# A four-mixer block on one core: bias rows spread by four transfers, memory tokens prepared in pieces, earlier splits of the last weights, another closing chain

## The chip, the cores and the metric

The kernel runs on one core of one Trainium2 chip. The metric is device microseconds (us) of one execution. The engines are named as in the profile: PE (matrix products), PEld (its weight loads), DVE (vector), ACT (scalar), POOL (GpSimd) and SP, whose queue (SPq) issues the transfers (DMA).

## The reference, cut to what matters

All inputs are fp32, one sequence of 512 tokens, model width 1024, 256 memory tokens.

```
h = _rmsnorm(x, norm_g[l])
p_fox, p_ssm, p_nsa, p_mem = _split(h @ w_in[l], [FOX_COLS, SSM_COLS, NSA_COLS, MEM_COLS])
mem_kv = _rmsnorm(mem, mem_norm_g[l]) @ w_mem_kv[l]
o = concatenate([_fox_mixer(p_fox, ..), _ssd_mixer(p_ssm, ..), _nsa_mixer(p_nsa, .., rel_bias_table), _mem_mixer(p_mem, mem_kv)])
x = x + o @ w_out[l]
return _rmsnorm(x, final_norm_g)
```

fox is causal attention with a decay, ssd a scan over state in four chunks of 128 tokens, nsa attention over compressed, selected and windowed keys with a bias taken from a table by distance, mem attention to the memory tokens. Inside ssd the lines that the change touches are

```
y = _ssd_chunked(xs * dt, dt * a, bh, ch)
y = y + xs * d_skip
yg = y * silu(z)
return _rmsnorm(yg by groups of 256, norm_g)
```

where a chunk's result is `cb @ x`, inside the chunk, plus `C @ prev * exp(acs)`, with `prev` the state that the chunks before left.

## The kernel before, in words

**Precision.** Every large product is made of three: each operand is split into a high part, rounded to a shorter format, and the low rest. A tile of weights (`raw`, 128x1024, 512 KB) arrives by a transfer on SP, ACT copies it into `wh` and POOL subtracts to get `wl` (`split`). `three` then issues `wh*hh`, `wh*hl` and `wl*hh`. Rings of three hold `raw`, `wh` and `wl`. The last output weights (`wo1`, eight halves) are split into `lh` and `ll`, which lie in the general store.

**Order.** `ORDER` lists 74 weight tiles. Tiles are taken in that order. While the Python code is run to emit instructions, a planner (`Clock`) keeps an estimated time for every engine, `Sched` and `Pipe` pick the next step by it: weight tiles are filled in where the pipeline steps of the mixers (fox, cmp, mem, pre, ssm, nsa, each a `Pipe` of stages) would wait. So the order of instructions on every engine is fixed when the program is built, and each engine takes its own list in order. `tt` puts an elementwise product on DVE or on POOL by the planner's estimate. `Store` counts the tiles that are free: 51 of 128x512 (`gs`) and 12 of 128x1024 (`bs`). A pipeline keeps some in reserve (RF, RM, RN, RS) and holds at most so many steps open (DF, DM, DN, DS).

**Start.** `proj_b("bv")` makes fox's values from the unscaled, unnormalised tokens `uh`/`ul` (ACT, DVE), tile by tile as `xt` arrives: per tile two row blocks k of 128, four token tiles each.

**Bias of nsa.** `rel_bias` makes eight rows `rv`, writes them to DRAM, and eight transfers DRAM to DRAM copy each row 128 times (`rows`, 328 KB each). Much later `bias_tile` reads the copies with a step that is one element shorter, so that each partition has a shifted row.

**Memory tokens.** `mem_r` and `prep_mem` normalise: `prm` on PE spreads a factor, DVE makes `mt`, ACT `mh`, POOL `ml`. `mem_v` multiplies them with the `mv` weights into `pmv`. In the list of things to do, the preparation is an entry (`memx`) right ahead of the first `mv`.

**The scan.** For each chunk stage s1 makes `pR`, `pG`, `pX` (and `pB`) on PE, two masks `m` from `pR` on DVE, `ce` and eight exponentials on ACT, `m*pG` on DVE, and `xdt`, `xde`. Then `pst` and `prev` (the state), `pY` on PE (32 products from the second chunk on), `yc` on DVE (four from `pY`, four times z), its squares `sq` on ACT, sums by `pn` on PE, and after `rsr`/`prs` the scaled `of`, split to `oh`/`ol`. `po` are the output products. `wo1` needs the scan's `oh`/`ol`.

**Close.** `out_last` adds the last `po` to `acc` by pieces, and `finish` squares on ACT with a running sum, adds it up through `fv` and `fw` (DVE), takes the power (`fr`, POOL), multiplies by the gain `fgn`, scales half on DVE and half on ACT, and two transfers write 128 tokens.

Every instruction is recorded at the line of one helper (L229 before, L231 after), so rows are told apart by tile names.

## Time and profile before

| | us |
|---|---|
| median of 3 runs | 564.74 (563.86 to 565.84) |
| the profiled execution | 564.22 |
| its span in the profile | 562.4 |
| PE busy in it | 545.1 (97%) |
| DVE, ACT, POOL busy | 335.2, 316.0, 228.0 |

The span is divided between times at which the engines work and short stretches at which PE does nothing. Times in the rows below count from the span's start. A timeline row has the start, the duration, the engine, the operation with what it writes and reads, how many such follow one another, and in brackets the idle time just ahead of it and what ended that.

### The profile page before, as it was taken

Reading aid. Unit: us, or ns where it says so; the run is one execution under the profiler, and the core shown is the slowest. Engines: PE = TensorE matmul, PEld = TensorE weight load, DVE = VectorE, ACT = ScalarE, POOL = GpSimd, SP = SyncE. Lnnn points to the kernel's source line nnn. Section 1 sums busy time; section 2 is a strip of 40 time slices with the busy share of each in tenths; the row PEclk is TensorE's granted clock in tenths of the full one; section 3 lists DMA queues with packets and bytes.
Section 4 is the critical chain, followed back from the end, with each engine's and each line's share of the span. In section 5 each row is a group of like instructions: output and inputs, shape, how many; then the busy total and the mean of one; then the engine's idle time right before and its main releaser. Section 6 shows DMA issues by size and latency. Waiting matters only on the chain.

```text
span 562.4 us, 8836 instructions
## 1 busy us (share of the span) xinstructions
PE 545.1 (97%) x3237; PEld 450.5 (80%) x3237; DVE 335.2 (60%) x891; ACT 316.0 (56%) x709; POOL 228.0 (41%) x145
## 2 busy tenths in 40 slices
PE   8999979999989999999999999999999999999993
PEld 4897858887867888888888888888888888888683
DVE  3566555665565354555646656777666556778654
ACT  5656534876456554556655657556656563527323
POOL 3495342332658334333131423333133313739433
PEclk9999979999989999999999999999999999999997
DMA  8772462212614232513221222442212211223012
GB/s 289 305 260 89 177 197 99 76 26 70 226 38 143 89 106 76 175 53 109 80 76 38 75 76 76 139 163 76 75 38 76 75 60 54 76 75 114 1 38 112
DMA packets 18919, 59.01 MB, mean 105 GB/s; under 512 B 2315, under 2 KB 2587, under 8 KB 18876
## 3 DMA queue, kind: packets, MB, share of 16 engines
...
q8 instruction: 25, 0.41, 0.3%
q14 instruction: 18, 0.15, 0.1%
...
## 4 chain that ended last, share of the span: by engine, by line
PE 84%; DVE 4%; DMA 3%; issue 3%; POOL 2%; ACT 2%; SPq 1%; POOLq 0%; ACTq 0%; DVEq 0%
PE pj L229 41%; PE po L229 12%; PE pO L229 7%; PE pT L229 6%; PE pb L229 6%; PE pS L229 5%; DMA raw<-in_wst 3%; PE pmv L229 2%; PE pW L229 1%; PE pY L229 1%; SPq L229 1%; DVE acc L229 1%; ACT sq L229 1%; POOL ll L229 1%; POOL fr L229 0%
## 5 line engine op out<-in xcount | busy, mean ns | idle before, releaser
L229 POOL TENSOR_TENSOR wl<-raw,wh 128x1024 fp32r<-128x1024 f32 (+1 forms) x72 | 172.2, 2396 | 283.4 <-ACT wh L229 262.6
L229 PE MATMUL pj<-hh,wh 128*128 128x512 f32 x352 | 144.4, 410 | 2.2 <-ACT wh L229 2.2
L229 PE MATMUL pj<-hh,wl 128*128 128x512 f32 x352 | 138.9, 395 | 1.2 <-POOL wl L229 1.2
L229 PE MATMUL pj<-hl,wh 128*128 128x512 f32 x352 | 138.7, 394 | 0.0
L229 ACT ACTIVATE wh<-raw 128x1024 fp32r<-128x1024 f32 (+1 forms) x72 | 74.9, 1042 | 21.5 <-DMA raw<-in_wst 14.4
L229 PEld LDWEIGHTS pj<-hh,wl 128*128 128x128 f32 x352 | 66.6, 189 | 16.7 <-POOL wl L229 1.9
L229 PEld LDWEIGHTS pj<-hh,wh 128*128 128x128 f32 x352 | 66.9, 190 | 15.9 <-ACT wh L229 2.6
L229 PEld LDWEIGHTS pj<-hl,wh 128*128 128x128 f32 x352 | 67.0, 190 | 10.7
L229 ACT ACTIVATE pN<-pN,nm 128x128 f32<-128x128 f32 (+7 forms) x96 | 45.3, 473 | 30.6 <-DVE nm L229 29.7
L229 PE MATMUL po<-wh,oh 128*128 128x512 f32 x96 | 39.4, 410 | 0.0
L229 PE MATMUL po<-wh,ol 128*128 128x512 f32 x96 | 37.6, 391 | 0.0
L229 PE MATMUL po<-wl,oh 128*128 128x512 f32 x96 | 37.5, 391 | 0.0
L229 ACT ACTIVATE pN<-pN,rs 128x128 f32<-128x128 f32 (+3 forms) x32 | 18.1, 564 | 29.0 <-DVE rs L229 29.0
L229 DVE TENSOR_SCALAR rs<-sm 128x3 f32<-128x3 f32 x32 | 11.9, 371 | 28.1 <-ACT pN L229 28.1
L229 DVE CUSTOM_DVE_ANT_0 pN<-pS,bt 128x128 f32<-128x128 f32 (+4 forms) x72 | 21.0, 329 | 12.1 <-PE pS L229 10.3
L229 ACT ACTIVATE pF<-pF,nm 128x128 f32<-128x128 f32 (+3 forms) x32 | 17.7, 554 | 14.6 <-DVE nm L229 14.6
L229 DVE SCALAR_TENSOR_TENSOR xs<-cb,cwh,xs 128x512 f32<-128x512 f32 x24 | 18.0, 752 | 11.5 <-ACT xs L229 10.9
L229 DVE TENSOR_TENSOR acc<-acc,po 128x512 f32<-128x512 f32 (+1 forms) x33 | 21.2, 665 | 5.4 <-PE po L229 5.4
L229 DVE COPY pt<-pT 128x512 f32<-128x512 f32 (+1 forms) x37 | 21.8, 599 | 3.1 <-PE pT L229 2.9
L229 PE MATMUL pT<-cst,pN 128*128 128x128 f32 x160 | 23.0, 275 | 0.0
L229 PE MATMUL pb<-wh,ul 128*128 128x512 f32 (+1 forms) x64 | 21.4, 347 | 0.8 <-DVE ul L229 0.8
L229 PEld LDWEIGHTS pT<-cst,pN 128*128 128x128 f32 x160 | 18.7, 140 | 4.3 <-issue 1.2
...
## 6 DMA issues: line engine op xcount, KB each, us to landing
...
```

The lines of the kernel that those rows point to most:

```text
L229: return f(*a, **k)
```

## The change

- `proj_b("bv")`: per tile the order of products is now hh, ul for the first row block, hh for the second, `wl` for the first, ul and `wl` for the second. Before, hh and ul alternated for both row blocks, then `wl`.
- Bias rows: four transfers of 656 KB (256 rows), two when `rv` is written, the others at nsa's steps 0 and 1. `bias_tile` is one transfer in place of two. `rel` follows `kc`, which is nine places later in `ORDER`.
- Memory tokens: a generator in `side`, stepped once each time an `mv` or `mk` tile is among the next three things to do. `mem_v` and `mk` run what is left of it.
- `wo1` weights may be split four tiles ahead (others two, as before).
- The scan: the factor 0.5 is moved into two small vectors, so that `yc` times z is a plain product which `tt` can place on POOL.
- Close: sums of pieces in one tile `fs`, one reduction, POOL multiplies the first half by the gain, one DVE instruction applies factor and gain to the second half, ACT scales the first. The end of a token tile is emitted behind the next tile's first addition. The last transfer is issued by ACT.
- Numbers: `ORDER`, depths, reserves and the biases of `tt` are others (two of ORDER's lines are shown), and the planner counts 2.0 us more for a PE step ahead of which PE stood for over 1.7 us.

```diff
-DF, DM, DN, DS = 4, 6, 3, 4
+DF, DM, DN, DS = 5, 3, 5, 3
...
-RF, RM, RN, RS = 3, 2, 2, 4
-
-SOON, LATER, WIDE = 0, 2500, 8000
+RF, RM, RN, RS = 4, 3, 2, 7
+
...
-    ("kc", 0), ("fq", 1), ("fg", 0), ("fk", 0), ("fk", 1), ("fq", 2), ("fg", 1), ("fk", 2),
...
+    ("fk", 0), ("fk", 2), ("vc", 0), ("fq", 3), ("fg", 0), ("fk", 1), ("fq", 1), ("fq", 2),
...
     def can_split():
         i = state["split"]
-        if i >= min(state["next"] + 2, len(ORDER)):
+        if i >= len(ORDER) or i >= state["next"] + (4 if ORDER[i][0] == f"wo{LAST}" else 2):
...
             ks_ = range(i * per, min((i + 1) * per, KT))
-            for x, w_ in (("h", h_), ("l", l_)):
-                for k in ks_:
-                    if name == "bv" and (i, x) in (((0, "h"), (0, "l"))[1:] + ((1, "h"),)):
-                        stat_x(k)
-                    ahead()
-                    if name == "bc" or i > 1:
-                        pump()
-                    cs = slice((k - i * per) * width, (k - i * per + 1) * width)
-                    for t in range(4):
-                        tk = slice(t * 128, (t + 1) * 128)
-                        if x == "h":
-                            T.matmul(pb[t][:, :width], uh[k][:, tk], w_[:, cs], start=k == 0, stop=False)
-                            T.matmul(pb[t][:, :width], ul[k][:, tk], w_[:, cs], start=False, stop=False)
-                        else:
-                            T.matmul(pb[t][:, :width], uh[k][:, tk], w_[:, cs], start=False, stop=k == KT - 1)
+            if name == "bv":
+                order = [(0, 0), (0, 1), (1, 0), (0, 2), (1, 1), (1, 2)]
+            else:
+                order = [(j, x) for j in range(len(ks_)) for x in (0, 1)] + [(j, 2) for j in range(len(ks_))]
+            for n_, (j, x) in enumerate(order):
+                k = ks_[j]
+                if name == "bv" and (i, n_) in ((0, 3), (0, 5), (1, 1), (1, 3)):
+                    stat_x(2 * i + n_ // (5 - 2 * i))
+                ahead()
+                if name == "bc" or i > 1:
+                    pump()
+                cs = slice(j * width, (j + 1) * width)
+                u, w_ = (ul if x == 1 else uh)[k], l_ if x == 2 else h_
+                for t in range(4):
+                    T.matmul(pb[t][:, :width], u[:, t * 128:(t + 1) * 128], w_[:, cs],
+                             start=k == 0 and x == 0, stop=k == KT - 1 and x == 2)
             done((h_, l_))
...
+    side = []
+
+    def memory(whole=False):
+
+        while side and side[0]:
+            if next(side[0], 1):
+                side[0] = None
+            if not whole:
+                break
+
     def soon(key):
+        if key[0] in ("mv", "mk") and (len(mh) or bg.room(4 + bg.kept(), 2)):
+            memory()
...
     def tile_a(key, sink, h=None, width=512):
         h_, l_ = get(key)
-        yield max(clock.ready([h_, l_]), clock.free_banks(1))
+        if h:
+            memory(True)
+        hi, lo = h if h else (hh, hl)
+        yield max(clock.ready([h_, l_, *hi, *lo]), clock.free_banks(1))
         p = PS("pj")
-        hi, lo = h if h else (hh, hl)
...
         cs = slice(c0, c0 + w)
-        sq, fs = G("sq", FT, w), SM("fs", 1)
-        A.activation(sq, a[:, cs], AF.Square, accum_out=fs)
+        if i == 0:
+            fin["s"] = SM("fs", 4)
+            V.memset(fin["s"], EPS)
+        fs = fin["s"]
+        sq = G("sq", FT, w)
+        A.activation(sq, a[:, cs], AF.Square, scale=D ** -0.5, accum_out=fs[:, i:i + 1])
         gs.drop()
-        if not last:
-            tt(LATER, out=a[:, cs], in0=a[:, cs], in1=g[:, cs], op=OP.mult)
-            if i == 0:
-                fin["v"] = SM("fv", 1)
-                V.tensor_scalar(out=fin["v"], in0=fs, scalar1=1.0 / D, scalar2=EPS, op0=OP.mult, op1=OP.add)
-            else:
-                V.scalar_tensor_tensor(out=fin["v"], in0=fs, scalar=1.0 / D, in1=fin["v"], op0=OP.mult, op1=OP.add)
+        if i == 0:
+            P.tensor_tensor(out=a[:, cs], in0=a[:, cs], in1=g[:, cs], op=OP.mult)
+        if last:
+            fin["end"] = t, i, fs
+
+    def end():
+        if "end" not in fin:
             return
+        t, i, fs = fin.pop("end")
+        a, g = acc[t], fin["g"]
         v, r = SM("fw", 1), SM("fr", 1)
-        V.scalar_tensor_tensor(out=v, in0=fs, scalar=1.0 / D, in1=fin["v"], op0=OP.mult, op1=OP.add)
+        V.tensor_reduce(out=v, in_=fs[:, 0:i + 2], axis=mybir.AxisListType.X, op=OP.add)
         P.tensor_tensor(out=r, in0=v, in1=nhalf[:, :1], op=OP.pow)
-        V.tensor_tensor(out=a[:, cs], in0=a[:, cs], in1=g[:, cs], op=OP.mult)
-        V.tensor_scalar(out=a[:, 0:512], in0=a[:, 0:512], scalar1=r, scalar2=None, op0=OP.mult)
-        Q.dma_start(out=out[t][:, 0:512], in_=a[:, 0:512])
-        A.activation(a[:, 512:1024], a[:, 512:1024], AF.Copy, scale=r)
+        V.scalar_tensor_tensor(out=a[:, 512:1024], in0=a[:, 512:1024], scalar=r, in1=g[:, 512:1024],
+                               op0=OP.mult, op1=OP.mult)
         Q.dma_start(out=out[t][:, 512:1024], in_=a[:, 512:1024])
+        A.activation(a[:, 0:512], a[:, 0:512], AF.Copy, scale=r)
+        (Q if t < 3 else nc.scalar).dma_start(out=out[t][:, 0:512], in_=a[:, 0:512])
...
             V.tensor_tensor(out=a, in0=a, in1=p[:, :w], op=OP.add)
+            end()
             finish(t, i, c0, w, i == len(pieces) - 1)
...
-    rows = [[dr.tile([128, RVW], FT, name=f"rows{j}_{a}") for a in range(2)] for j in range(4)]
+    rows = [dr.tile([2, 128, RVW], FT, name=f"rows{j}") for j in range(4)]
...
-        for j in range(4):
-            for a in range(2):
-                src = rv[4 * a + j:4 * a + j + 1, :]
-                Q.dma_start(out=rows[j][a], in_=bass.AP(tensor=src.tensor, offset=src.offset,
-                                                              ap=[[0, 128], [1, RVW]]))
-            yield 0
+        yield 0
         gs.drop(2)
         bs.drop()
+        spread(0)
+        spread(1)
+
+    def spread(j):
+        src = rv[j:j + 1, :]
+        Q.dma_start(out=rows[j], in_=bass.AP(tensor=src.tensor, offset=src.offset, ap=[[4 * RVW, 2], [0, 128], [1, RVW]]))
 
     def bias_tile(j):
         t = B4("bt", [128, 2, BTW])
-        for a in range(2):
-            src = rows[j][a]
-            Q.dma_start(out=t[:, a, :], in_=bass.AP(tensor=src.tensor, offset=src.offset + 127,
-                                                          ap=[[RVW - 1, 128], [1, BTW]]))
+        src = rows[j]
+        Q.dma_start(out=t, in_=bass.AP(tensor=src.tensor, offset=src.offset + 127,
+                                       ap=[[RVW - 1, 128], [128 * RVW, 2], [1, BTW]]))
         return t
...
                     bts[j + 1] = bias_tile(j + 1)
+                if j < 2:
+                    spread(j + 2)
...
-                V.scalar_tensor_tensor(out=yc[:, jc], in0=xs[j][:, ck], scalar=v_d[:, j:j + 1], in1=po[:, jc],
+                V.scalar_tensor_tensor(out=yc[:, jc], in0=xs[j][:, ck], scalar=hd[:, j:j + 1], in1=po[:, jc],
                                        op0=OP.mult, op1=OP.add)
             for j in range(4):
                 jc = slice(j * 128, (j + 1) * 128)
-                V.scalar_tensor_tensor(out=yc[:, jc], in0=yc[:, jc], scalar=0.5, in1=R["z", j][:, ck],
-                                       op0=OP.mult, op1=OP.mult)
+                tt(0, out=yc[:, jc], in0=yc[:, jc], in1=R["z", j][:, ck], op=OP.mult)
...
     def mem_v():
+        memory(True)
         for i in range(4):
             h_, l_ = get(("mv", i))
-            yield max(clock.ready([h_, l_]), clock.free_banks(2) if i == 0 else 0.0)
+            yield max(clock.ready([h_, l_, *mh, *ml]), clock.free_banks(2) if i == 0 else 0.0)
...
-    rm = mem_r()
+    side.append(prep_mem(mem_r()))
...
-        if key[0] in ("mv", "mk") and not seen_x:
-            bg.add(("memx", 0), prep_mem(rm))
-            seen_x = True
```

SP's queue where the bias rows are copied. First before: `rv` are the eight rows, `rows` the copies, `raw` weight tiles.

```order
L229 DMA raw<-in_wst 128x1024
L229 DMA rv<-rvs 8x328
L229 DMA rv<-rvt 8x328
L229 DMA rows_0_487<-rv 128x656
L229 DMA rows_1_488<-rv 128x656
L229 DMA rows_0_489<-rv 128x656
L229 DMA rows_1_490<-rv 128x656
L229 DMA rows_0_491<-rv 128x656
L229 DMA rows_1_492<-rv 128x656
L229 DMA rows_0_493<-rv 128x656
L229 DMA rows_1_494<-rv 128x656
```

The same place after; `xst` are small transfers of compressed keys.

```order
L231 DMA raw<-in_wst 128x1024 x4
L231 DMA xst<-kv 64x511
L231 DMA xst<-kv 64x512
L231 DMA raw<-in_wst 128x1024 x6
L231 DMA rv<-rvs 8x328
L231 DMA rv<-rvt 8x328
L231 DMA rows_487<-rv 256x1x656
L231 DMA rows_488<-rv 256x1x656
L231 DMA raw<-in_wst 128x1024
L231 DMA xst<-kv 64x511
```

The copies stand behind nine more weight tiles, and two transfers are left here.

PE's queue at the memory tokens, before. `pcm` are products of the compression, `prm` and `pmv` as above.

```order
L229 MATMUL pcm_1573<-w1_1511,xp_1519 64x128
L229 MATMUL pcm_1573<-w1_1515,xp_1525 64x128
L229 MATMUL prm_1609<-cst_98,rmr_546 128x128 x2
L229 MATMUL pmv_1640<-wh_1437,mh_1613 128x512
L229 MATMUL pmv_1640<-wl_1438,mh_1613 128x512
L229 MATMUL pmv_1640<-wh_1437,ml_1612 128x512
```

After, at `prm` (`pj` are products of ordinary weight tiles):

```order
L231 MATMUL pj_1429<-hl_435,wh_1206 128x512
L231 MATMUL pj_1429<-hh_413,wl_1207 128x512
L231 MATMUL prm_1523<-cst_98,rmr_542 128x128 x2
L231 MATMUL pj_1543<-hh_276,wh_1292 128x512
L231 MATMUL pj_1543<-hl_298,wh_1292 128x512
```

and at `pmv`:

```order
L231 MATMUL pj_1632<-hh_413,wh_1425 128x512
L231 MATMUL pj_1632<-hl_435,wh_1425 128x512
L231 MATMUL pj_1632<-hh_413,wl_1426 128x512
L231 MATMUL pmv_1673<-wh_1534,mh_1527 128x512
L231 MATMUL pmv_1673<-wl_1535,mh_1527 128x512
L231 MATMUL pmv_1673<-wh_1534,ml_1526 128x512
```

Between `prm` and `pmv` there now stand 48 products `pj` (two weight tiles) and 32 of `pcm`.

PE's queue at the last chunk of the scan, before, from the `pst` ahead of that chunk's `pR` to the first `pY` of the third chunk:

```order
L229 MATMUL pst<-xde,bt 128x256 x2
L229 MATMUL pR<-bd,cgs 128x512 x2
L229 MATMUL pG<-xs 128x128 x2
L229 MATMUL pX<-cst,xs 128x128 x4
L229 MATMUL po<-wh,oh 128x512
L229 MATMUL po<-wl,oh 128x512
L229 MATMUL po<-wh,ol 128x512
L229 MATMUL po<-wh,oh 128x512
L229 MATMUL po<-wl,oh 128x512
L229 MATMUL po<-wh,ol 128x512
L229 MATMUL prs<-cst,rsr 128x128 x2
L229 MATMUL pY<-m,xdt 64x128 x2
```

This `pY` is followed by 12 `po`, the last chunk's `pY`, 15 `po`, and then `pn`. After, from the last `po` ahead of the last chunk's `pR`:

```order
L231 MATMUL po<-wh,ol 128x512
L231 MATMUL pR<-bd,cgs 128x512 x2
L231 MATMUL pG<-xs 128x128 x2
L231 MATMUL pX<-cst,xs 128x128 x4
L231 MATMUL pst<-xde,bt 128x256 x2
L231 MATMUL pY<-m,xdt 64x128 x2
L231 MATMUL pY<-ce,prev 64x128 x2
```

The pair of `pY` rows stands eight times, four for the third chunk and four for the last, and behind them:

```order
L231 MATMUL pY<-m,xdt 64x128 x2
L231 MATMUL pY<-ce,prev 64x128 x2
L231 MATMUL pn<-ones,sq 128x1 x2
L231 MATMUL po<-lh,oh 128x512
L231 MATMUL po<-ll,oh 128x512
L231 MATMUL po<-lh,ol 128x512
```

The `po` with `lh` are the first of `wo1`. Ahead of the first row of after stand the third chunk's `pR`, `pG`, `pX`, `pB` and eight more `po`; between the two chunks' `pR` there were 30 `po` before and are nine now, and no product of another kind stands between the last `pR` and `wo1`.

DVE's queue there, before, from the last chunk's masks on:

```order
L229 TENSOR_TENSOR m<-pR,umask 128x512 x2
L229 TENSOR_TENSOR xdt<-pX,dtv 128x512
L229 TENSOR_TENSOR m<-m,pG 128x512 x2
L229 SCALAR_TENSOR_TENSOR of<-yc,vec,prs 128x128 x4
L229 TENSOR_TENSOR ol<-of,oh 128x512
L229 SCALAR_TENSOR_TENSOR yc<-xs,vec,pY 128x128 x4
L229 SCALAR_TENSOR_TENSOR yc<-yc,sg 128x128 x4
L229 TENSOR_TENSOR sq<-sq 128x128
L229 SCALAR_TENSOR_TENSOR yc<-xs,vec,pY 128x128 x4
L229 SCALAR_TENSOR_TENSOR yc<-yc,sg 128x128 x4
```

After, from the third chunk's `xdt` on:

```order
L231 TENSOR_TENSOR xdt<-pX,dtv 128x512
L231 TENSOR_TENSOR xde<-xdt,dte 128x512
L231 TENSOR_TENSOR m<-m,pG 128x512 x2
L231 TENSOR_TENSOR acc<-acc,po 128x512 x2
L231 TENSOR_TENSOR m<-pR,umask 128x512 x2
L231 TENSOR_TENSOR xdt<-pX,dtv 128x512
L231 TENSOR_TENSOR m<-m,pG 128x512 x2
L231 TENSOR_TENSOR prev<-prev,decR 128x512
L231 TENSOR_TENSOR prev<-prev,pst 128x512
L231 SCALAR_TENSOR_TENSOR yc<-xs,hd,pY 128x128 x4
L231 TENSOR_TENSOR yc<-yc,sg 128x128
```

The last chunk's masks stand behind the third chunk's `m*pG`, and the third chunk's `yc` behind the last chunk's `m*pG` and `prev`.

## Rows read from the trace of the kernel before

**Rows 1.** The chain of work that ended last, from the page: shares of the span by engine.

```profile
PE 84%; DVE 4%; DMA 3%; issue 3%; POOL 2%; ACT 2%; SPq 1%; POOLq 0%; ACTq 0%; DVEq 0%
```

**Rows 2.** Busy time of the engines by stretch: start and end, length, then for PE, PEld, DVE, ACT, POOL the busy us and in brackets the instructions; then PE's granted clock as a share of full speed, the share of the DMA engines, and GB/s.

```profile
75.00:77.50 2.50, 0.68 (x4) 0.22 (x2) 0.00 (x0) 0.74 (x1) 0.00 (x0) 1.00 0.52 199
77.50:85.00 7.50, 5.92 (x14) 4.25 (x15) 4.00 (x5) 3.50 (x5) 7.02 (x3) 0.54 0.44 143
...
159.00:163.00 4.00, 1.70 (x9) 1.06 (x8) 3.97 (x10) 2.13 (x4) 1.57 (x2) 1.00 0.00 0
163.00:166.50 3.50, 3.50 (x12) 2.95 (x12) 1.65 (x7) 2.75 (x7) 3.50 (x4) 0.51 0.00 0
166.50:529.00 362.50, 362.50 (x2240) 304.44 (x2240) 220.76 (x639) 206.37 (x496) 139.03 (x83) 1.00 0.25 85
529.00:531.70 2.70, 2.14 (x10) 1.32 (x9) 2.15 (x5) 2.56 (x6) 2.32 (x3) 1.00 0.00 0
531.70:535.20 3.50, 3.45 (x9) 1.73 (x7) 0.82 (x3) 0.54 (x2) 3.50 (x3) 0.51 0.00 0
```

**Rows 3.** Timeline of PE and of DVE in the first tile of `bv`.

```profile
8.09 0.40 PE L229 MATMUL pb<-wh,ul 128*128 128x512 f32 x1
8.32 0.43 PE L229 MATMUL pb<-wh,uh 128*128 128x512 f32 x1
9.55 0.50 PE L229 MATMUL pb<-wh,ul 128*128 128x512 f32 x1 [0.80 <-DVE ul L229]
...
8.23 1.92 DVE L229 SCALAR_TENSOR_TENSOR ul<-xt,vec,uh 128x512 fp32r<-128x512 f32 x2 [1.70 <-ACT uh L229]
```

**Rows 4.** Timeline of SP's queue where the bias rows are copied.

```profile
58.76 5.75 SPq L229 DMA_DIRECT2D rows<-rv  x8
64.61 1.29 SPq L229 DMA_DIRECT2D raw<-in_wst  x1
```

**Rows 5.** Timeline where the weights behind them land.

```profile
76.76 1.06 ACT L229 ACTIVATE wh<-raw 128x1024 fp32r<-128x1024 f32 x1 [5.88 <-DMA raw<-in_wst]
...
77.87 0.80 PE L229 MATMUL pj<-hh,wh 128*128 128x512 f32 x1 [2.18 <-ACT wh L229]
```

**Rows 6.** Timeline of PE, DVE and POOL at the memory tokens.

```profile
161.35 0.50 PE L229 MATMUL pmv<-wh,mh 128*128 128x512 f32 x1 [1.63 <-ACT mh L229]
...
162.76 0.56 PE L229 MATMUL pmv<-wh,ml 128*128 128x512 f32 x1 [0.68 <-POOL ml L229]
...
159.78 3.21 DVE L229 SCALAR_TENSOR_TENSOR mt<-mt,vec,prm 128x256 f32<-128x256 f32 x8
...
161.43 4.99 POOL L229 TENSOR_TENSOR ml<-mt,mh 128x512 fp32r<-128x512 f32 x4 [6.59 <-issue]
```

**Rows 7.** Timeline of PE and POOL at the last weight tile of `wo1`.

```profile
531.23 0.50 PE L229 MATMUL po<-ll,oh 128*128 128x512 f32 x1 [0.52 <-POOL ll L229]
...
529.90 5.44 POOL L229 TENSOR_TENSOR ll<-raw,lh 128x512 fp32r<-128x512 f32 x4
```

**Rows 8.** Timeline of the scan's last chunk: PE's block `pR` to `pX` (the next `po` ends it), the state `prev`, the masks and the last `m*pG`; PE's `pY` of that length, from its first row to the next `po`; `yc`, its squares, and their sums.

```profile
514.58 0.81 PE L229 MATMUL pR<-bd,cgs 128*128 128x512 f32 x2
514.71 0.97 DVE L229 TENSOR_TENSOR prev<-prev,decR 128x512 f32<-128x512 f32 x1
...
515.78 0.69 DVE L229 TENSOR_TENSOR prev<-prev,pst 128x512 f32<-128x512 f32 x1
...
516.03 0.48 PE L229 MATMUL po<-wh,oh 128*128 128x512 f32 x1
...
516.39 1.28 DVE L229 TENSOR_TENSOR m<-pR,umask 128x512 f32<-128x512 f32 x2
...
520.73 0.69 DVE L229 TENSOR_TENSOR m<-m,pG 128x512 f32<-128x512 f32 x1 [0.49 <-ACT m L229]
...
522.89 0.44 PE L229 MATMUL pY<-m,xdt 128*64 128x128 f32 x4
...
524.78 0.50 PE L229 MATMUL po<-wh,oh 128*128 128x512 f32 x1
...
526.71 1.12 DVE L229 SCALAR_TENSOR_TENSOR yc<-xs,vec,pY 128x128 f32<-128x128 f32 x4
...
528.67 0.63 ACT L229 ACTIVATE sq<-yc 128x512 f32<-128x512 f32 x1 [2.20 <-DVE yc L229]
...
529.38 0.56 POOL L229 TENSOR_TENSOR sq<-sq 128x128 f32<-128x128 f32 x1 [2.27 <-ACT sq L229]
```

**Rows 9.** The tile `xde`: one DVE operation with two inputs, three times; ns shortest, median and longest.

```profile
L229 DVE TENSOR_TENSOR xde<-xdt,dte x3: 693/1298/1811, 470.8 to 508.4; 128x512 f32<-128x512 f32 x3
```

**Rows 10.** Timeline of the close, from PE's last product.

```profile
553.28 0.28 PE L229 MATMUL po<-lh,ol 128*128 128x256 f32 x1
...
555.06 0.15 DVE L229 TENSOR_SCALAR fv<-fs 128x1 f32<-128x1 f32 x1 [0.85 <-ACT sq L229]
...
556.31 0.41 DVE L229 TENSOR_TENSOR acc<-acc,po 128x256 f32<-128x256 f32 x1
...
557.60 0.59 POOL L229 TENSOR_TENSOR fr<-fw,nhalf 128x1 f32<-128x1 f32 x1 [0.55 <-DVE fw L229]
...
558.23 0.49 DVE L229 TENSOR_SCALAR acc<-acc,fr 128x512 f32<-128x512 f32 x1 [0.43 <-POOL fr L229]
558.74 0.81 SPq L229 DMA_DIRECT2D out<-acc  x2
```

More of the change, by code (lines that the diff above doesn't have):

```diff
@@ L144, in note @@
                 self.tiled = tiled
+            if start > self.t[eng] + 1700:
+                took += 2000
         elif eng == "SP":
-            took = 430
+            took = 720 if self.box(out) == (0, 1, 0, 1) else 430
         elif eng == "ACT":
@@ L169, in note @@
             nbytes = 4 * self.size(out) * out.ap[0][1]
-            self.dma = max(self.dma, done) + nbytes / 340
+            self.dma = max(self.dma, done) + nbytes / (170 if took > 430 else 340)
             done = self.dma + 2100
@@ L263, in step @@
         item = self.todo[0]
-        if item[2] is None:
-            for key, *_ in self.todo[:2]:
-                self.soon(key)
+        for key, *_ in self.todo[:3]:
+            self.soon(key)
         try:
@@ L618, in block_kernel @@
     gs.drop(16)
+    mh, ml = [], []
     o_f, o_hl, last = {}, {}, [0]
@@ L623, in ready @@
         g, b = TAKES[key[0]]
+        if key[0] in ("mv", "mk") and not mh:
+            g, b = g + 4, b + 2
         if key[0] in ("ks", "kw") and kx or key[0][:2] == "wo" and acc:
@@ L1372, in s1 @@
                 xde = G("xde")
-                V.tensor_tensor(out=xde.rearrange("p (h d) -> p h d", h=8),
-                                in0=xdt.rearrange("p (h d) -> p h d", h=8), in1=hb(dte, c), op=OP.mult)
+                tt(SOON, out=xde.rearrange("p (h d) -> p h d", h=8),
+                   in0=xdt.rearrange("p (h d) -> p h d", h=8), in1=hb(dte, c), op=OP.mult)
             for g in range(2):
@@ L1604, in block_kernel @@
     adders.update(extra)
-    seen_mv = seen_x = False
+    seen_mv = False
     for key in ORDER[7:]:
-        if key[0] in ("mv", "mk") and not seen_x:
-            bg.add(("memx", 0), prep_mem(rm))
-            seen_x = True
         if key == ("kc", 0):
@@ L1629, in block_kernel @@
         bg.fill()
+    end()
 def _bucket(dist):
```

12 lines of the change are left out of this document (7 added, 5 removed), and 12 rows, old and new, of the table ORDER.

## The prediction

> **What bounds the kernel now.** I read the chain of waits first. PE has 84% of it, no other engine more than 4% [rows 1]: the time is PE's work plus the places where PE stands or runs slowly. So I looked for these places in the busy times by stretch. In the long middle PE is busy for all of 362.5 us at full clock [rows 2]; the loss lies in a few short stretches and at the two ends. In a stretch I count as lost PE's idle time, and of its busy time the share that the granted clock lacks. Three stretches come out:
>
> - 75.0 to 85.0: idle 1.82 + 1.58, and 5.92 busy at 0.54 loses 2.7, sum 6.1 us. PE waits for `wh`, ACT had waited 5.88 us for a weight tile [rows 5]. That tile was issued at 64.61, behind eight copies of bias rows which took SP 5.75 us [rows 4].
> - 159.0 to 166.5: idle 2.30, and 3.50 at 0.51 loses 1.7, sum 4.0. PE waits 1.63 for `mh` and 0.68 for `ml`: DVE, ACT and POOL prepare memory tokens that PE wants at once [rows 6].
> - 529.0 to 535.2: idle 0.61, and 3.45 at 0.51 loses 1.7, sum 2.3. `ll` of the last tile is made while PE is there [rows 7]; modelled ends of products hide a little, I take 2.5.
>
> A clock near 0.5 of 2.4 GHz is the lower level, 1.2; each time it follows an idle gap of PE in the same stretch or the one before. At the start one wait for `ul` moves a product from 0.23 to 1.23 us behind the last [rows 3]. At the end 9.1 us pass from PE's last product at 553.28 to the span's end, 562.4.
>
> **The change part by part.** *Start.* The product at 8.32 is the ninth, the one at 9.55 the tenth and the first to read `ul` of the second block, which DVE has ready just ahead of it (the first of the two from 8.23) [rows 3]. In the new order that `ul` is first read by the seventeenth product, at 8.32 + 8 × 0.23 = 10.2, so the wait of 1.0 goes. The weight tiles that follow then have 1.0 less room, so between 0 and 1.0 is gained; I take 1.0, since nothing is added to ACT or POOL there.
>
> *Bias rows.* Two transfers of 656 KB at this place carry half the bytes, so SP and the queue behind them should be done in about half of the time that the eight took: the weight tile that landed 12.1 us after its issue (64.61 to 76.76 less a little) would take some 6. By the order, with 0.23 a product, its split is due about 17 us after the place of the copies and its use about 33. That covers it twice. The other two transfers stand at nsa's steps 0 and 1, alone. Gain 6.1; with the cover gone, up to 6.1 comes back. `bias_tile` in one transfer saves SP an issue; SP bounds nothing there.
>
> *Memory tokens.* Between `prm` and the first `pmv` PE has 48 products `pj`, 48 × 0.23 = 11.0 us, and 32 `pcm`. The preparation took from 159.78 (DVE) to 166.4 (end of POOL's four `ml`), 6.6 us, and POOL's weight splits for two tiles can be put between. It is hidden with over 4 us to spare: gain 4.0. If POOL were late after all, that comes back.
>
> *Last weights.* Made up to four tiles ahead, `ll` is ready well before PE is there: gain 2.5.
>
> *The price: the last chunks.* `wo1` held early takes 16 tiles of the general store, and with the larger reserve of the scan (RS 7) the last two chunks start late. The order shows what that does: behind the third chunk's `pR` stand nine `po`, the last chunk's `pR`, both `pY`, `pn`, then `wo1`. PE has nothing else to run while two chunks go one behind the other through DVE and ACT, where before 12 and 15 `po` stood in between. Durations of [rows 8], with zero at the third chunk's `pR`:
>
> 1. PE: `pR` to `pX` 1.45 twice, `pB` 0.15, nine `po` 2.05, `pst` 0.7 (about three products): 5.8. Two `pY` of 1.9 and `pn` would end at 9.75 if nothing had to be waited for.
> 2. DVE: the third chunk's masks start at about 1.0 (behind `of` and `ol` in its order). From masks to the end of the last `m*pG` it is 516.39 to 521.42, 5.03. ACT also copies `bt`, some 0.2 more: end 6.2. Two additions `acc` of 0.65 follow: 7.5.
> 3. Then the last chunk's masks: 7.5 + 5.03 = 12.5. `prev` 514.71 to 516.47, 1.76: 14.3. The last `pY` reads it and runs from 14.3 to 16.2, or to 18.1 at half clock.
> 4. Only then, in DVE's order, the third chunk's `yc`: 14.3 + 1.1. Of its products by z three go to POOL, 0.56 each like the sums of squares there, from 14.65 to 16.35. Squares on ACT 0.7: 17.05. Sum on POOL 0.56: 17.6. `pn`, and `wo1` can start at 17.8 to 18.3.
>
> That is 8.0 to 8.5 behind 9.75; I take 8.2. PE stands about 6 us in one piece in it, so a stretch at half clock follows; the three of before lasted 3.5 to 7.5 us and lost 1.7 to 2.7 each [rows 2]. Part of it lies under `pY`, which is waited out anyway. I add 1.5, from 0 to 3.5. Sum 9.7, between 8 and 12; more, by 1 to 1.5, if DVE comes to the third chunk's masks late because four `acc` stand ahead.
>
> Eleven of sixteen products by z are on POOL. The one row that bears on the two engines together is `xde`, two inputs from SBUF, the same shape three times: 693, 1298 and 1811 ns [rows 9]; something holds it up by as much as 1.1. I count no such hold-up in the steps above. The Trainium skill (SBUF — State Buffer, section "SBUF: two separate sides") says that DVE and POOL share one pair of ports, that a DVE operation with two inputs from SBUF or a POOL operation takes it for its whole length, and that the other is blocked entirely. The spread of `xde` agrees. By that rule two of the three products on POOL could each cost DVE 0.56 more, and the forecast would be 1.1 later.
>
> *Close.* Before, the last addition on DVE stood behind `fv`, which waited for ACT, and started at 556.31, 3.0 after PE's last product [rows 10]. Now no such wait is ahead of it: it can start 0.5 after (product 0.28, and a little). From addition to the second half's scaling it was 556.31 to 558.23, 1.9, the same steps now (squares, a sum, power); the scaling is one operation with gain, about 0.2 longer. The transfer issue 0.4 later is saved, since ACT issues the other. So 2.5 − 0.2 + 0.4 less a little for the power on POOL, which also holds a product by the gain: 2.4, between 1.8 and 2.7.
>
> *Sum.* Gains 1.0 + 6.1 + 4.0 + 2.5 + 2.4 = 16.0, price 9.7. The profiled execution is 564.22 (span 562.4, 1.8 around it), so 557.9. The median is 0.52 above it: **558.4**.
>
> **The rivals.**
>
> *A, the forecast:* 555 to 561.5.
>
> *B, the last chunks cost less* (3 to 7): the 5.03 from masks to the last `m*pG` holds waits, since other work of that time stood between (`ce` on ACT among it). If a chunk takes 3.5 with nothing beside it, twice 1.5 is saved, and with a shorter gap the half clock: 558.4 − 3.0 − 1.5 = 553.9, so 551 to 555.5. Against it: `ce` is made in every chunk, and `prev` stood ahead of the masks in the row, so the 5.03 holds none of it.
>
> *C, a smaller stall elsewhere*, where preparation in pieces makes `wl` late (POOL has 5.0 of `ml` beside 2 × 2.4 of `wl` in 11 us), or the shorter start leaves a `bv` tile late. It gives back 3 to 6: 561.5 to 564.5. Against it: POOL was idle for 14.5 us at a time in the profile.
>
> *D, the copies still block a weight tile:* the bytes are the same in all, and a transfer of 656 KB may hold the queues as long as two of 328. One such stall as before gives back 6.1: 564.5, no change. That is also the case in which the change doesn't do what it says.
>
> *E, slower:* the same mechanism at three places, the pair and the two single transfers in nsa's steps, each ahead of a weight tile. At 6.1 a place it is 558.4 + 18.3 = 576.7; it decides from the second place on, with 570.6 for two. For it: 5.88 us of waiting were seen behind eight copies. Against it: each single transfer is a quarter of that, and three weight tiles are kept in the ring.
>
> **How the numbers follow.** A 0.60, B 0.11, C 0.12, D 0.09, E 0.08. A measurement of this kernel can tell about 0.3%, 1.7 us, from no change. Faster by more than that is below 563.05: A, B and most of C, 0.80. Within it: D and the rest of C, 0.12. Slower: E, 0.08. The range leaves out E, part of D and the lower half of B: 552 to 564.
>
> **What would show it.** Right: in the changed profile the first `bv` tile without the gap of 1.23; ACT without a wait of several us for a weight tile behind `rows`; `pmv` without waits; no wait of `po` for `ll`; the span's end 6.5 to 7 us after PE's last product. And one stretch near the end, just ahead of the first `po` with `lh`, in which PE idles for 8 us between `pY` and `pn` with DVE on `m*pG` and `prev`, followed by a granted clock near 0.5. Wrong: `pY` of the last chunk released at once (B), PE idle behind `rows` (D, E), or `wl` late beside `ml` (C).

## The result, and the profile after

| | before | changed |
|---|---|---|
| median, us | 564.46 (563.86 to 565.84, 4 runs) | 571.83 (570.55 to 574.34, 4 runs) |
| ratio, 95% interval | | 1.0132 (1.0091 to 1.0174) |
| profiled execution (span) | 564.22 (562.4) | 571.07 (568.9) |

The change made the kernel 1.3% slower; 558.4 was forecast, and 552 to 564 as the range. The chain that ended last, from the page of the changed kernel, answers to [rows 1]:

```profile
PE 79%; DVE 7%; ACT 6%; DMA 6%; issue 1%; POOL 0%; SPq 0%; POOLq 0%; DVEq 0%; ACTq 0%
```

DMA has doubled, ACT tripled, and PE lost 5 points. The stretches of the changed kernel, columns as in [rows 2]:

```profile
143.00:146.00 3.00, 0.80 (x7) 0.41 (x6) 0.00 (x0) 0.00 (x0) 0.00 (x0) 0.95 0.82 233
146.00:160.00 14.00, 4.22 (x27) 3.66 (x28) 0.00 (x0) 1.80 (x3) 4.46 (x6) 0.52 0.67 240
160.00:521.80 361.80, 361.80 (x2235) 304.12 (x2234) 217.92 (x620) 209.14 (x495) 152.64 (x99) 1.00 0.27 91
521.80:538.40 16.60, 11.46 (x101) 9.84 (x99) 12.25 (x22) 8.99 (x24) 9.86 (x10) 0.90 0.00 0
```

Counted as there (idle, and of busy time what the clock lacks), 143 to 160 lost 2.2 + 9.8 + 2.0 = 14.0 us. The miss is 13.4 us (571.83 against 558.4), so this is its size; the other terms that came out otherwise add up to −1.5 (below). The stretch is the one of the bias rows, which now lies here instead of at 75 to 85. SP's queue, answering to [rows 4]:

```profile
121.70 6.35 SPq L231 DMA_DIRECT2D rows<-rv  x2
128.15 10.18 SPq L231 DMA_DIRECT2D raw<-in_wst  x1
...
138.46 4.99 SPq L231 DMA_DIRECT2D xst<-kv  x2
```

The two `rows` were issued in 6.35 us, and then the issue of one weight tile took 10.18 us, where the median of all is 0.33. Meanwhile the DMA engines had little to do:

```profile
129.00:135.00 6.00, 6.00 (x44) 4.61 (x43) 2.48 (x11) 3.01 (x10) 0.93 (x1) 1.00 0.13 51
```

13% of 16 engines is 2.1 engines, at 51 GB/s. In the trace's packet records these are some 58 packets of 2,624 bytes (one bias row) in 3 us, each of about 0.11 us. At the same stage before, the copies reached 307 in 3 us, at 71% of the engines:

```profile
66.00:69.00 3.00, 3.00 (x15) 2.10 (x14) 0.97 (x2) 1.93 (x4) 0.00 (x0) 1.00 0.71 269
```

The chain of waits has the weight tile behind them, with start and duration:

```profile
128.15 25.90 DMA raw<-in_wst
```

25.9 us from issue to landing, where before it was 12.1. The packet records show why it came so late past engines that were idle. Of the tile's 128 packets (4,096 bytes each) 112 start between 139.0 and 141.0, right behind SP's issue. No further packet of that size starts before 144.8, and the tile lands at 154.05, just after the last of 512 row packets has started (152.35). The 16 that are missing are what two engines of 16 would carry, so they fit a rest that stood behind the copies on the same two engines; the records don't name the engine. ACT and PE there:

```profile
154.41 1.06 ACT L231 ACTIVATE wh<-raw 128x1024 fp32r<-128x1024 f32 x1 [15.11 <-DMA raw<-in_wst]
155.37 0.84 ACT L231 COPY pt<-pT 128x256 f32<-128x256 f32 x2
...
155.78 2.82 PE L231 MATMUL pO<-pt,fv 128*64 128x128 f32 x22 [11.97 <-ACT pt L231]
```

ACT's queue stood 15.1 us at the `wh` of that tile. Behind it in the same queue was `pt`, a copy that fox's `pO` needs, so PE stood for `pO`, which has nothing to do with the tile. After 12 us of idling PE ran at 0.52 of its clock.

The other places. In the start, answering to [rows 3]:

```profile
7.08 1.08 PE L231 MATMUL pb<-wh,ul 128*128 128x512 f32 x4
9.21 1.19 PE L231 MATMUL pb<-wh,uh 128*128 128x512 f32 x4 [1.05 <-ACT uh L231]
...
8.44 1.36 ACT L231 ACTIVATE uh<-xt,vec 128x512 fp32r<-128x512 f32 x2 [0.42 <-DMA xt<-in_xT]
```

The wait for `ul` is gone and PE waits for `uh` of the second block instead, whose `xt` lands late. In fox a new wait of 1.4 us appears. It comes with the new order of tiles: run e12 below, the kernel before with the first 22 tiles in that order, has it too.

```profile
78.67 0.44 PE L231 MATMUL pT<-cst,pF 128*128 128x128 f32 x2 [1.42 <-ACT pF L231]
```

`pmv` and `ll` are not waited for any more. The last chunks (PE, then DVE and ACT), answering to [rows 8]:

```profile
532.62 0.44 PE L231 MATMUL pY<-m,xdt 128*64 128x128 f32 x4 [2.93 <-DVE m L231]
535.28 0.70 PE L231 MATMUL pY<-ce,prev 128*64 128x128 f32 x4 [2.21 <-DVE prev L231]
...
538.36 0.61 PE L231 MATMUL pn<-ones,sq 128*128 128x1 f32 x4
...
528.78 1.28 DVE L231 TENSOR_TENSOR m<-pR,umask 128x512 f32<-128x512 f32 x2
...
533.05 0.69 DVE L231 TENSOR_TENSOR m<-m,pG 128x512 f32<-128x512 f32 x1 [0.48 <-ACT m L231]
...
534.45 0.69 DVE L231 TENSOR_TENSOR prev<-prev,pst 128x512 f32<-128x512 f32 x1
535.05 1.12 DVE L231 SCALAR_TENSOR_TENSOR yc<-xs,hd,pY 128x128 f32<-128x128 f32 x4
536.08 0.40 DVE L231 TENSOR_TENSOR yc<-yc,sg 128x128 f32<-128x128 f32 x1
...
536.83 0.63 ACT L231 ACTIVATE sq<-yc 128x512 f32<-128x512 f32 x1 [3.81 <-POOL yc L231]
```

PE waits 2.9 us for the last chunk's `m*pG` and 2.2 for `prev`; the third chunk's `yc` starts only at 535.05, behind both, as the order had it. The stretch 521.8 to 538.4 lost 5.1 idle and 1.2 by the clock: 6.3. And the close, answering to [rows 10]:

```profile
562.18 0.28 PE L231 MATMUL po<-lh,ol 128*128 128x256 f32 x1
...
562.50 0.42 DVE L231 TENSOR_TENSOR acc<-acc,po 128x256 f32<-128x256 f32 x1 [0.28 <-PE po L231]
...
564.54 0.75 DVE L231 SCALAR_TENSOR_TENSOR acc<-acc,fr,fgn 128x512 f32<-128x512 f32 x1 [0.89 <-POOL fr L231]
565.29 0.40 ACTq L806 DMA_DIRECT2D out<-acc  x1
```

The last addition starts 0.3 us after PE's last product, where it was 3.0, and the span ends 6.7 us after it, where it was 9.1.

### The profile page after: what moved, and what is told of

It is laid out like the page before. It is cut to its first block, busy times and chain, and to the rows that moved or that the text cites. A ratio compares the mean times of both kernels' runs of the same rounds, so it can differ in the third digit from the quotient of the medians.

```text
span 568.9 us, 8824 instructions
## 1 busy us (share of the span) xinstructions
PE 540.7 (95%) x3237; PEld 449.8 (79%) x3237; DVE 332.1 (58%) x869; ACT 317.6 (56%) x712; POOL 236.4 (42%) x159
## 4 chain that ended last, share of the span: by engine, by line
PE 79%; DVE 7%; ACT 6%; DMA 6%; issue 1%; POOL 0%; SPq 0%; POOLq 0%; DVEq 0%; ACTq 0%
PE pj L231 35%; PE po L231 15%; PE pO L231 6%; PE pb L231 6%; PE pT L231 5%; DMA raw<-in_wst 5%; PE pS L231 4%; PE pmv L231 2%; PE pW L231 1%; ACT pF L231 1%; PE pY L231 1%; DMA xt<-in_xT 1%; DVE Rl L231 1%; ACT M L231 1%; ACT wh L231 1%
## 5 line engine op out<-in xcount | busy, mean ns | idle before, releaser
L231 DVE SCALAR_TENSOR_TENSOR sg<-sg,pj 128x512 f32<-128x512 f32 x16 | 11.0, 688 | 31.9 <-ACT sg L231 31.9
L231 PE MATMUL pO<-pt,fv 128*64 128x128 f32 x160 | 13.3, 302 | 12.0 <-ACT pt L231 12.0
L231 DVE COPY pt<-pT 128x512 f32<-128x512 f32 (+1 forms) x32 | 19.6, 618 | 7.2 <-PE pT L231 7.0
```

The source lines that it names most:

```text
L231: return f(*a, **k)
```

## The experiments

Medians, all against the kernel before on the same chip (its medians there 563.75 to 564.87); e2 and e7 ran twice each, the others four times or more.

| run | what | us | ratio, 95% interval |
|---|---|---|---|
| e1_rows128 | changed, copies outermost | 558.01 | 0.9878 (0.9851 to 0.9905) |
| e2_before_two | before, two rows outermost | 606.36 | 1.0744 (1.0707 to 1.0782) |
| e3_before_close | before, new close | 562.16 | 0.9958 (0.9941 to 0.9974) |
| e4_rows128_split3 | e1, three tiles ahead | 557.90 | 0.9888 (0.9864 to 0.9911) |
| e5_rows128_split2 | e1, two tiles ahead | 557.01 | 0.9880 (0.9861 to 0.9899) |
| e6_rows128_rs4 | e1, RS 4 | 557.36 | 0.9884 (0.9866 to 0.9901) |
| e7_rows8 | changed, one transfer, 8 outermost | 557.35 | 0.9886 (0.9860 to 0.9911) |
| e8_rows128_memwhole | e1, memory tokens in one piece | 570.00 | 1.0108 (1.0077 to 1.0138) |
| e9_before_split4 | before, four tiles ahead | 571.28 | 1.0113 (1.0086 to 1.0141) |
| e10_rows128_ztail | e1, wo3 behind z | 562.02 | 0.9966 (0.9948 to 0.9984) |
| e11_rows128_oldtail | e1, end as before | 559.62 | 0.9929 (0.9906 to 0.9953) |
| e12_close_late | before, new close, copies later | 564.11 | 0.9994 (0.9974 to 1.0013) |

**The shape of the copies.** The theory: the outermost dimension of a transfer sets how many engines share it, and the change made that 2. The rival: 1.3 MB block the weights in any shape.

```diff
-    rows = [dr.tile([2, 128, RVW], FT, name=f"rows{j}") for j in range(4)]
+    rows = [dr.tile([128, 2, RVW], FT, name=f"rows{j}") for j in range(4)]
...
-... ap=[[4 * RVW, 2], [0, 128], [1, RVW]]))
+... ap=[[0, 128], [4 * RVW, 2], [1, RVW]]))
...
-                                       ap=[[RVW - 1, 128], [128 * RVW, 2], [1, BTW]]))
+                                       ap=[[2 * RVW - 1, 128], [RVW, 2], [1, BTW]]))
```

> The changed kernel with one thing other: the four transfers of bias rows have the 128 copies as their outermost dimension instead of the two rows; same bytes, same places, the order of instructions on every engine is that of the changed kernel. Theory (shape): a transfer with two entries outermost is carried by about two of the 16 DMA engines (58 packets of 2624 bytes in 3 us, 51 GB/s, in the changed kernel's trace), so the weight tile behind it landed 25.9 us after its issue and PE stood 12 us, about 14 us lost with the clock. With 128 outermost the two first transfers end in some 6 us, no wait of ACT for that tile over 2 us, and 555 to 559 us. Rival (bytes): 1.3 MB at this place block the weights whatever their shape: 565 to 572.

558.01, 13.8 us below the changed kernel, by the order of three numbers in an access pattern. SP and ACT there, and two stretches at the end, in the columns of [rows 2]:

```profile
121.97 1.26 SPq L231 DMA_DIRECT2D rows<-rv  x2
123.32 0.56 SPq L231 DMA_DIRECT2D raw<-in_wst  x1
...
126.67 1.06 ACT L231 ACTIVATE wh<-raw 128x1024 fp32r<-128x1024 f32 x1
...
515.60:519.64 4.04, 0.78 (x12) 0.29 (x6) 2.33 (x5) 3.52 (x10) 2.49 (x2) 1.00 0.00 0
519.64:529.90 10.26, 8.37 (x42) 7.20 (x43) 5.30 (x17) 1.26 (x2) 4.00 (x8) 0.50 0.01 2
```

The copies are issued in 1.26 us, the tile behind them at 123.32, and its split at 126.67 waits for nothing. The rival falls.

The same shape put into the kernel before:

```diff
-            for a in range(2):
-                src = rv[4 * a + j:4 * a + j + 1, :]
-                Q.dma_start(out=rows[j][a], in_=bass.AP(tensor=src.tensor, offset=src.offset,
-                                                              ap=[[0, 128], [1, RVW]]))
+            src = rv[j:j + 1, :]
+            Q.dma_start(out=rows[j], in_=bass.AP(tensor=src.tensor, offset=src.offset,
+                                                 ap=[[4 * RVW, 2], [0, 128], [1, RVW]]))
```

> The kernel before with its eight transfers of bias rows made as four with two entries outermost, at their place. Theory (shape): four transfers at about 51 GB/s in all take some 50 us, the weights behind them land that late, and PE stands for 20 to 40 us: 585 to 610. Rival (bytes, or the place in the program): the bytes are the same, so 562 to 568.

606.36, and the slow carrying for all four transfers (SP, ACT, and the stretch 68 to 104):

```profile
58.97 33.45 SPq L229 DMA_DIRECT2D rows<-rv  x4
...
118.01 1.06 ACT L229 ACTIVATE wh<-raw 128x1024 fp32r<-128x1024 f32 x1 [47.12 <-DMA raw<-in_wst]
...
68.00:104.00 36.00, 7.69 (x34) 6.01 (x32) 4.58 (x8) 2.55 (x5) 0.00 (x0) 0.67 0.13 50
```

SP alone took 33 us to issue them, and ACT waited 47 us for a weight tile, at again 13% of the engines and 50 GB/s. So neither the place in the program nor the rest of the change matters to it.

Eight entries outermost, all rows in one transfer:

```diff
+        Q.dma_start(out=rows, in_=bass.AP(tensor=src.tensor, offset=src.offset, ap=[[RVW, 8], [0, 128], [1, RVW]]))
```

> The changed kernel with all bias rows copied by one transfer at the first place, eight entries outermost, 2.6 MB; some weight tiles and products stand a little otherwise around it. Theory (as many streams as there are entries outermost): about 200 GB/s, some 230 packets of 2624 bytes in 3 us, done in 13 us, the weight tile behind it lands within 17 us and PE hardly waits: 556 to 561. Rival (the bytes in one place block): 563 to 572. Rival (the outermost dimension does not set it, it was two transfers at a time that were slow): about 50 GB/s, done in 50 us, over 590.

557.35. SP's issue, and a stretch of the copy:

```profile
121.32 0.77 SPq L231 DMA_DIRECT2D rows<-rv  x1
...
124.00:127.00 3.00, 3.00 (x27) 2.33 (x26) 1.58 (x8) 2.65 (x8) 0.00 (x0) 1.00 0.49 172
```

49% of 16 engines is 7.8, at 172 GB/s; in the packet records it then settles at 218 to 231 packets in 3 us, about four times the 58 that two entries gave. So 2 and 8 entries have about as many engines, and 2.6 MB at once hurt no one at this width. The Trainium skill has this as a rule (DMA: Bandwidth & Descriptors, section "Rules for kernel authors"): the slowest dimension that isn't 1 sets over how many of the 16 engines a transfer is split, and an outermost dimension of fewer than 16 entries holds it to at most so many. The traces agree, with 2.1 and 7.8 engines busy by the time that the packets took. The prediction did not weigh that rule against the diff.

**The close** alone, in the kernel before: `finish`, `end` and the calls of `end` as in the change.

```diff
-        sq, fs = G("sq", FT, w), SM("fs", 1)
...
+        fs = fin["s"]
+        sq = G("sq", FT, w)
...
+            end()
             finish(t, i, c0, w, i == len(pieces) - 1)
```

> The kernel before with the closing chain alone of the change. Theory: the last addition no longer stands behind a wait of DVE for ACT, and the end comes 6.7 us after PE's last product instead of 9.1: 562.1 (561.8 to 562.7). Rival: the first half's product by the gain, now always on POOL, delays POOL's power or ACT, and it is 564 to 565.

562.16, 2.7 us below before: as expected, and the forecast's 2.4 holds.

**The last chunks.** Is it the early split that delays them, and can PE be given other products there? First e1 with three tiles ahead:

```diff
-        if i >= len(ORDER) or i >= state["next"] + (4 if ORDER[i][0] == f"wo{LAST}" else 2):
+        if i >= len(ORDER) or i >= state["next"] + (3 if ORDER[i][0] == f"wo{LAST}" else 2):
```

> The kernel with 128 entries outermost, and weights of the last output projection split at most three tiles ahead instead of four; the order differs from that kernel only from the third chunk of the scan on, where output products now stand between the chunks. Theory (the last chunks run back to back and PE waits about 7 us for them): 6 to 8 us below the kernel with 128 entries outermost, 547 to 552. Rival (PE would wait there in any order, for the scan's chain): within 2 us of it.

557.90, no gain. The wait at `pY` is gone, as planned, and another has come (PE, POOL):

```profile
532.29 0.71 PE L231 MATMUL prs<-cst,rsr 128*128 128x128 f32 x4 [3.07 <-POOL rsr L231]
533.33 0.69 PE L231 MATMUL pn<-ones,sq 128*128 128x1 f32 x4 [0.33 <-DVE sq L231]
...
530.27 1.26 POOL L231 TENSOR_TENSOR acc<-acc,fgn 128x512 f32<-128x512 f32 x1 [1.65 <-ACT sq L231]
531.50 0.74 POOL L231 TENSOR_TENSOR rsr<-rsv,nhalf 128x2 f32<-128x2 f32 x1
```

PE waits 3.1 us for `prs`; its `rsr` stands on POOL behind `acc` times `fgn`, the product that the new close always puts on POOL. Two tiles ahead, and, as another kernel, four tiles with the smaller reserve:

```diff
-        if i >= len(ORDER) or i >= state["next"] + (4 if ORDER[i][0] == f"wo{LAST}" else 2):
+        if i >= len(ORDER) or i >= state["next"] + 2:
```

```diff
-RF, RM, RN, RS = 4, 3, 2, 7
+RF, RM, RN, RS = 4, 3, 2, 4
```

> The kernel with 128 entries outermost, weights of the last output projection split at most two tiles ahead, as before the change; the order differs only from the third chunk of the scan on. With three ahead the wait of PE for the scan's products was gone, but PE waited 3.1 us for the factor of the third chunk (rsr on POOL, behind the closing chain of the first 128 tokens) and the time was the same. Here 7 us of products stand between the sums of the third chunk and its factor, where with three ahead there were 3.6. Theory (PE only lacks products of its own at the right places): 3 to 7 us below the kernel with four ahead at 558.0, 551 to 555. Rival (some chain through the other engines takes the place of each one removed): 556 to 559.

> The kernel with 128 entries outermost and the scan's reserve of tiles RS 4, as before the change, with weights still four tiles ahead; the order differs only from the third chunk on. First products of the last projection come between the two chunks, 4 us of them, and the chunks' own products 2 us apart. If the larger reserve made the last chunks late: 3 to 6 us below 558.0, 552 to 555. If the early split alone made it: 557 to 559, the chunks' chain still waits.

557.01 and 557.36: at most 1 us below e1, which the intervals do not separate. So neither the early split nor the larger reserve, taken back by itself, gives the loss back. In e5 PE waits 1.2 us for the last sums, 1.0 and 0.8 for `oh`, and runs at half clock after that; in e6 3.0 for `rsr` and 1.1 for `oh`. Two other orders of the end:

```diff
-    ("z", 2), ("wo3", 0), ("wo3", 1), ("xb", 6), ("z", 0), ("xb", 1), ("xb", 7), ("z", 1), ("z", 3),
+    ("z", 2), ("xb", 6), ("z", 0), ("xb", 1), ("xb", 7), ("z", 1), ("z", 3), ("wo3", 0), ("wo3", 1),
```

and, from the 43rd tile on, all in the order of before, with

```diff
-DF, DM, DN, DS = 5, 3, 5, 3
+DF, DM, DN, DS = 5, 3, 5, 4
...
-RF, RM, RN, RS = 4, 3, 2, 7
+RF, RM, RN, RS = 4, 3, 2, 4
...
+        if i >= len(ORDER) or i >= state["next"] + 2:
```

> The kernel with 128 entries outermost, with the two tiles wo3 0 and 1 of the weight order moved behind the last of z and xb; so the scan starts earlier in PE's work, and the third chunk's pY has 12 us of products ahead of it, the last chunk's 6. Theory (PE lacks products at the right places): only the last chunk's sums are waited for, 3 to 4 us, 553 to 556. Rival (some chain through the other engines takes the place of each one removed, as with two and three tiles ahead and with the smaller reserve): 556 to 558.5.

> The kernel with 128 entries outermost and, from the 43rd weight tile on, the order of before, with two tiles ahead, reserve 4 and depth 4 for the scan as before; the close and the fillings of z on POOL are those of the change. The scan's chunks stand earlier again: the last pR has 31 us of products behind it, 8 of them between its pY and its sums. Theory: PE waits 1.5 us for the last factor and 2 to 3 for oh behind it, little else, 552 to 555.5. Rival: 556 to 558.5, as above.

562.02 and 559.62, both slower than e1, and above the theory's range and the rival's alike. In e10 PE waits 2.4 us for the last sums, and a wait of 3.1 us opens ahead of a `pO` of the compressed keys, where no expectation had one. In e11 PE waits 3.3 for `rsr`, again behind `acc` times `fgn`, and 1.9 for `oh` (PE, of e10 and then of e11):

```profile
443.86 0.69 PE L231 MATMUL pO<-ct,vcm 96*64 96x128 f32 x4 [3.14 <-DVE ct L231]
539.07 0.99 PE L231 MATMUL pn<-ones,sq 128*128 128x1 f32 x4 [2.41 <-DVE sq L231]
...
539.80 1.22 PE L220 MATMUL prs<-cst,rsr 128*128 128x128 f32 x4 [3.27 <-POOL rsr L220]
```

So in five orders of the end the wait that was seen went, and another link of the same chain (masks, `pY`, sums, factor, `oh`) took its place. That is the mechanism of the rivals; their times were met in e4 to e6 and missed in e10 and e11.

What the early split does by itself, in the kernel before:

```diff
-        if i >= min(state["next"] + 2, len(ORDER)):
+        if i >= len(ORDER) or i >= state["next"] + (4 if ORDER[i][0] == f"wo{LAST}" else 2):
```

> The kernel before with one thing other: weights of the last output projection may be split four tiles ahead instead of two; the order differs only from the third chunk of the scan on. The wait of po for ll goes (2.5 us with the clock). But the last chunk's pR now stands some 20 us of PE's products ahead of the end where 38.7 us passed before, and its pY follows with nothing of length between. Theory (the early split itself delays the last chunk and PE waits for it): PE waits 5 to 6 us ahead of that pY and 2 to 3 us ahead of the last products, 567 to 573. Rival (it is the other numbers of the change, reserves and order, and the early split alone is harmless): 561 to 564.

571.28, 7.5 us slower, at the two places that were expected, ahead of the last `pY` and of the last products (PE):

```profile
538.76 0.71 PE L229 MATMUL prs<-cst,rsr 128*128 128x128 f32 x4 [2.31 <-POOL rsr L229]
541.69 0.70 PE L229 MATMUL pY<-m,xdt 128*64 128x128 f32 x4 [2.22 <-DVE m L229]
...
556.96 0.79 PE L229 MATMUL po<-lh,oh 128*128 128x512 f32 x1 [3.87 <-ACT oh L229]
```

2.3 us for the third chunk's factor, 2.2 for the last masks, 3.9 for the last `oh`. The split four ahead removes a loss of 2.5 us and makes one of about 10. This holds for the kernel before; in the changed kernel e5 took the same split out and gained at most 1.0 us, so there it is not shown to be the cause.

**The memory tokens.** e1, with the preparation in one piece:

```diff
-        if key[0] in ("mv", "mk") and (len(mh) or bg.room(4 + bg.kept(), 2)):
-            memory()
```

> The kernel with 128 entries outermost, with the memory tokens prepared in one piece ahead of the first product that needs them, not step by step; some 4 us of other products stand between where 13 stood. Theory (the stall of before comes from the 6.6 us that the preparation takes): PE waits 2 to 3 us there and runs at half clock after it, 560 to 562.5. Rival (it is hidden in any case): 557 to 559.

570.00, 12.0 us above e1 and more than either theory had. The wait isn't where it was looked for (PE, then DVE):

```profile
173.92 1.63 PE L231 MATMUL pO<-pt,fv 128*64 128x128 f32 x12 [8.10 <-DVE pt L231]
...
167.97 2.44 DVE L231 SCALAR_TENSOR_TENSOR mt<-mt,vec,prm 128x256 f32<-128x256 f32 x6
171.09 1.57 DVE L231 TENSOR_TENSOR ml<-mt,mh 128x512 fp32r<-128x512 f32 x1 [0.68 <-ACT mh L231]
172.59 0.86 DVE L231 SCALAR_TENSOR_TENSOR mt<-mt,vec,prm 128x256 f32<-128x256 f32 x2
173.37 1.01 DVE L231 COPY pt<-pT 128x256 f32<-128x256 f32 x2
```

PE stands 8.1 us at fox's `pO`, for `pt`, which DVE copies only at 173.37, behind eight `mt` and one `ml`. In one piece the preparation blocks a queue that others need.

**The place alone.** The kernel before with the new close, the first 22 weight tiles as in the changed kernel, and the eight transfers as they were:

```diff
-    ("kc", 0), ("fq", 1), ("fg", 0), ("fk", 0), ("fk", 1), ("fq", 2), ("fg", 1), ("fk", 2),
...
+    ("fk", 0), ("fk", 2), ("vc", 0), ("fq", 3), ("fg", 0), ("fk", 1), ("fq", 1), ("fq", 2),
+    ("fg", 1), ("kc", 0), ("mq", 0), ("fg", 2), ("fk", 3), ("nq", 0),
```

> The kernel before with the new closing chain (562.2 by itself) and the first 22 weight tiles in the changed kernel's order, so that the bias rows are copied nine weight tiles later than before; the eight transfers of 328 KB, 128 copies outermost, stay as they were, all at one place. The end of the program is that of before. Theory (the copies' stall goes by the later place alone, with the new shape not needed): 6.1 us gained, 1.6 lost where fox's transposes are now waited for, 556.5 to 558.5, as fast as the best of the other versions, since the last chunks keep their products. Rival (eight transfers in one place stall the weights wherever they stand): 561 to 564.

564.11 (SP, PE):

```profile
122.84 6.67 SPq L218 DMA_DIRECT2D rows<-rv  x8
130.03 0.36 SPq L218 DMA_DIRECT2D raw<-in_wst  x1
...
171.13 0.79 PE L218 MATMUL pmv<-wh,mh 128*128 128x512 f32 x1 [6.53 <-ACT mh L218]
```

The copies' stall did go: the tile behind them is issued in 0.36 us and PE waits for none there. But `pmv` now waits 6.5 us for `mh`, where it was 1.6 [rows 6]: DVE comes to `mt` only at 169.56, behind fox's `pF` among others, so in the new order the two meet there. The theory was right about the copies and missed that, so the total came out just above the rival's range of 561 to 564.

## Why the prediction was wrong, by its own steps

- **Bias rows, the step that failed:** "Two transfers of 656 KB at this place carry half the bytes, so SP and the queue behind them should be done in about half of the time". Time was taken from bytes. The number of engines that carry a transfer, about 2 of 16 here against about 11 before, was left out, though the diff shows the pattern with 2 in front of 128. Measured: 25.9 us to land, not 6; PE lost 14.0, not 0. The cover was read rightly: ACT came to the split of that tile at 139.3, 17.6 us after the place of the copies, where 17 had been worked out. Left out was that ACT, stopped there, also holds back `pt`, so PE stood from 143.8 on for work that has no need of the tile. Rivals D and E had "the copies still block a weight tile", with 6.1 a place, taken from the stall of before; one place cost 14.0. That E's 570.6 for two places lies near 571.83 is luck. The two single transfers later are as narrow (some 57 packets in 3 us) and cost PE nothing: it is busy without a gap from 160 to 521.8. Shown by e1, e2 and e7.
- **Start:** forecast 1.0. In the traces the second tile starts at 13.10 to 13.53 in the five with the old order and at 12.42 to 13.13 in the nine with the new; means 13.3 and 12.8, so 0.5. `uh`, from the landing of `xt`, is the next releaser.
- **Memory tokens:** forecast 4.0 and hidden; in the changed kernel `pmv` waits for nothing. The step is right, and by e8 more hangs on it than the prediction had.
- **Last weights:** the wait for `ll` went, as forecast (2.5).
- **Last chunks:** forecast 9.7. The chain came in the order that was worked out: waits for `m*pG`, then `prev`, with `yc` behind. 6.3 were lost in the changed kernel and 5.1 + 4.2 = 9.3 in e1, which has the same order; the idle times are the same 5.1, and the difference is the clock: 0.90 over 16.6 us is 3.3 at half speed in one, and in the other it is 10.3. So the term was mis-sized: 8.2 were forecast for the delay, with PE standing about 6 in one piece, and 1.5 for the clock; PE stood 5.1 in two pieces, and the clock took 1.2 in one execution and 4.2 in the other. Rival B fails: from masks to the last `m*pG` the last chunk took 4.96 (528.78 to 533.74), as much as the 5.03 of before. By e9 the early split alone brings such a loss in the kernel before; what brings it in the changed kernel stays open, since e5 and e6 took the split and the reserve back one at a time and gained at most 1.0.
- **The products by z on two engines.** The product by z that DVE makes beside POOL's three took 0.40 (536.08), where before four took 0.89; POOL's three took 1.33. By the rule of the Trainium skill on the ports that the two share (SBUF — State Buffer, section "SBUF: two separate sides") the prediction's estimate was 1.1 more; 0.1 to 0.2 shows. That doesn't go against the rule: DVE's product ends 0.14 us after POOL's second, and before the change the two long `xde` end 0.55 us after a `wl` on POOL, while the short one has no work of POOL beside it. The estimate counted two products of POOL against DVE; here one stood in its way, and not for long.
- **Close:** forecast 2.4, measured 2.4 in the trace (9.1 to 6.7) and 2.7 in e3.
- **Rival C:** a smaller stall elsewhere did come, 1.4 us in fox, but by neither of the ways that C names (`wl` late, or a late tile of `bv`).

The sum by terms: 557.9 + 14.0 (copies) + 0.5 (start) + 1.4 (fox) − 3.4 (last chunks) = 570.4, against 571.07 in the profiled execution. Without the one failing step the forecast stands: e1 is 558.01, forecast 558.4. That it comes so near is in part luck: by terms e1 would be 557.9 + 0.5 + 1.4 − 0.4 = 559.4, and its profiled execution took 559.80; its others took 556.40 to 559.06, at granted clocks of 0.994 down to 0.987.

The quickest versions are e5, e6 and e7, 557.0 to 557.4, 1.2% below before. What stays open is whether an order exists that gives the last chunk's chain cover at every link; none of the five does.
